# Splitting the first load of a rotary-embedding kernel into two DMAs

## The chip, the cores and the metric

One core of one Trainium2 chip. The metric is the device time of the kernel in microseconds (us); every run computes the whole reference.

## The reference

Rotary position embedding on interleaved pairs, fp32 in and out. `x` is 8 x 2048 x 16 x 64 (batch, position, head, element; 67.1 MB), `cos` and `sin` are 2048 x 32.

```python
x_pairs = x.reshape(batch, seq_len, num_heads, head_dim // 2, 2)
x1, x2 = x_pairs[..., 0], x_pairs[..., 1]
out1 = x1 * cos - x2 * sin
out2 = x1 * sin + x2 * cos
out = np.stack([out1, out2], axis=-1).reshape(batch, seq_len, num_heads, head_dim)
```

## The kernel before

One tile holds one batch. Its 2048 positions are dealt to 128 partitions, 16 (`K`) consecutive positions to each, so a partition's row is 16 x 1024 elements: 64 KB in DRAM as fp32, 32 KB on the chip as bf16. There are five such buffers (`NX`) for the eight batches.

`load` (L58) is a DMA from the GpSimd (POOL) queue that casts fp32 to bf16 on its way; `store` (L61) is one that casts back. `rotate` is three VectorE (DVE) operations on a tile: the product with the sine table into a scratch tile `qt` (L76), the product with the cosine table in place (L77), and the sum of the one and the pair-swapped other (L82).

The order of each engine's work is written out by hand (`manual_schedule`):

- SP issues three DMAs first (L86 to L88): the head, that is the first four (`HEAD`) positions of every partition's row of batch 0, as fp32 into a staging tile; then the two tables, in rows of 2 KB per partition. Much later it issues the store of the last four positions of the last batch (L126).
- POOL issues the loads at once: the other 12 positions of batch 0, batches 1 to 3 whole, and batch 4 in two parts, 14 positions and 2.
- ScalarE (ACT) casts the head to bf16 into batch 0's tile (L95). VectorE builds the tables in bf16 (L97 to L99, the sine table first), then rotates batch 0 in two parts (4 positions, 12 positions) and the others whole.
- The store of batch 0 is held back until the first part of batch 4's load has landed: ACT copies one element of it (`gate`, L112) and then one of tile 0 onto itself (L113), and the store waits for the latter. `mark` (L110) makes POOL wait in the same way for the rest of batch 4 before it stores batch 1.
- From batch 1 on, POOL issues the store of batch b and then the load of batch b + 4 into the buffer that batch b - 1 left, which waits until that batch's store has landed.
- At the end, ACT waits for batch 6's store (L124), casts the last four positions to fp32 (L125), and SP stores them.

The staging tile of the head, the scratch tile `qt` and the staging tile of the end share one buffer (tag `work`).

Of the kernel before, what the change touches and what calls it, by code (L numbers as in the profile page):

```python
# [2 lines left out]

# [4 lines left out]


@with_exitstack  # L10
def kernel(
    ctx: ExitStack,
    tc: tile.TileContext,
    x: bass.AP,
    cos: bass.AP,
    sin: bass.AP,
    out: bass.AP,
):
    nc = tc.nc
    fp32 = mybir.dt.float32  # L20
    bf16 = mybir.dt.bfloat16
    mult = mybir.AluOpType.mult
    add = mybir.AluOpType.add

    B, S, H, D = x.shape
    P = 128
    K = S // P
    KP = 16
    D2 = D // 2
    HD = H * D  # L30
    NX = 5
    HEAD = 4
    TAIL = 4
    LAST = 2


    x_t = x.rearrange("b (p k) h d -> b p k (h d)", p=P, k=K)
    out_t = out.rearrange("b (p k) h d -> b p k (h d)", p=P, k=K)
    cos_t = cos.rearrange("(p k) c -> p (k c)", p=P, k=K)
    sin_t = sin.rearrange("(p k) c -> p (k c)", p=P, k=K)  # L40

    consts = ctx.enter_context(tc.tile_pool(name="consts", bufs=1))
    xpool = ctx.enter_context(tc.tile_pool(name="xpool", bufs=NX))
    stage = ctx.enter_context(tc.tile_pool(name="stage", bufs=1))

    cos_sb = consts.tile([P, K * D2], fp32)
    sin_sb = consts.tile([P, K * D2], fp32)
    c_tab = consts.tile([P, K, D], bf16)
    s_tab = consts.tile([P, K, D], bf16)

    gate = consts.tile([1, 1], bf16)
    mark = consts.tile([1, 1], bf16)
    tiles = {}

    def load(b, k0=0, k1=K):
        if b not in tiles:
            tiles[b] = xpool.tile([P, K, HD], bf16, name="xt")
        nc.gpsimd.dma_start(out=tiles[b][:, k0:k1], in_=x_t[b, :, k0:k1])  # L58

    def store(b, k1=K):  # L60
        nc.gpsimd.dma_start(out=out_t[b, :, :k1], in_=tiles[b][:, :k1])  # L61

    def rotate(b, k0, k1):
        nk = k1 - k0
        xp = tiles[b][:, k0:k1]
        qt = stage.tile([P, KP, HD], bf16, name="qt", tag="work")

        def rows(a):
            return a.rearrange("p k (h e) -> p k h e", h=H, e=D)

        def tab(a):
            return dataclasses.replace(
                a, offset=a.offset + k0 * D, ap=[a.ap[0], [D, nk], [0, H], [1, D]]
            )

        nc.vector.tensor_tensor(out=rows(qt[:, :nk]), in0=rows(xp), in1=tab(s_tab), op=mult)  # L76
        nc.vector.tensor_tensor(out=rows(xp), in0=rows(xp), in1=tab(c_tab), op=mult)  # L77
        q_swap = dataclasses.replace(
            qt, offset=qt.offset + 1, ap=[qt.ap[0], [2, nk * HD // 2], [-1, 2]]
        )  # L80
        x3 = xp.rearrange("p k (a j) -> p (k a) j", j=2)
        nc.vector.tensor_tensor(out=x3, in0=x3, in1=q_swap, op=add)  # L82

    with tc.manual_schedule():
        head = stage.tile([P, TAIL, HD], fp32, name="st", tag="work")
        nc.sync.dma_start(out=head[:, :HEAD], in_=x_t[0, :, :HEAD])  # L86
        nc.sync.dma_start(out=cos_sb, in_=cos_t)
        nc.sync.dma_start(out=sin_sb, in_=sin_t)  # L88
        load(0, HEAD)
        for b in range(1, NX - 1):  # L90
            load(b)
        load(NX - 1, 0, K - LAST)
        load(NX - 1, K - LAST)

        nc.scalar.copy(out=tiles[0][:, :HEAD], in_=head[:, :HEAD])  # L95
        s2 = s_tab.rearrange("p k (i j) -> p (k i) j", j=2)
        nc.vector.tensor_copy(out=s2[:, :, 0], in_=sin_sb)  # L97
        nc.vector.tensor_scalar_mul(s2[:, :, 1], sin_sb, -1.0)  # L98
        nc.vector.tensor_copy(  # L99
            out=c_tab.rearrange("p k (i j) -> p (k i) j", j=2),  # L100
            in_=cos_sb.to_broadcast([P, K * D2, 2]),
        )
        for b in range(B):
            if b == 0:
                rotate(b, 0, HEAD)
                rotate(b, HEAD, KP)
            else:
                rotate(b, 0, KP)
            if b == 1:
                nc.gpsimd.tensor_copy(out=mark, in_=tiles[NX - 1][:1, K - 1, :1])  # L110
            if b == 0:
                nc.scalar.copy(out=gate, in_=tiles[NX - 1][:1, K - LAST - 1, :1])  # L112
                nc.scalar.copy(out=tiles[0][:1, 0, :1], in_=tiles[0][:1, 0, :1])  # L113
            if b < B - 1:
                store(b)

            if b >= 1 and b - 1 + NX < B:
                load(b - 1 + NX)
        store(B - 1, K - TAIL)

        tail = stage.tile([P, TAIL, HD], fp32, name="st", tag="work")
        nc.scalar.copy(out=tiles[B - 2][:1, 0, :1], in_=tiles[B - 1][:1, K - 1, :1])  # L124
        nc.scalar.copy(out=tail, in_=tiles[B - 1][:, K - TAIL :])  # L125
        nc.sync.dma_start(out=out_t[B - 1, :, K - TAIL :], in_=tail)  # L126


# [1 line left out]
_INS = ['x', 'cos', 'sin']  # L130
_OUTS = [((8, 2048, 16, 64), 'float32')]


# [23 lines left out]
```

## Time and profile before

| | us |
|---|---|
| median of three runs | 316.58 (316.47 to 316.62) |
| the profiled execution's own time | 316.51 |
| its span, first to last instruction | 314.7 |
| VectorE busy | 210.4 (67%) |
| ScalarE busy | 8.9 (3%) |
| GpSimd busy | 15.2 (5%) |
| head DMA (L86), issue to landing | 14.5 |
| cosine DMA (L87), issue to landing | 31.8 |
| sine DMA (L88), issue to landing | 51.3 |

The DMA work is in two queues: the one that GpSimd's DMAs use (q0 in the profile, software descriptors) moves 97.52 MB in 2448 packets, and the one that SP's use (q1, hardware descriptors) 4.72 MB in 576. A packet is one partition's row or one semaphore update; its bytes are counted as written, so a load that casts counts half of what it reads. Both queues run on the same 16 DMA engines, so each engine has eight rows of every DMA.

### The profile page before, as it was taken

What the parts mean: (1) busy time and instruction counts of PE and PEld (TensorE: products, weight loads), DVE (VectorE), ACT (ScalarE), POOL (GpSimd) and SP (SyncE); (2) the same over time, 40 slices, a digit from 0 to 9 for tenths busy, and PEclk for the clock granted to TensorE, in tenths of its full rate; (3) what the DMA queues carried; (4) which work ended last, traced back from release to release, by engine and by line L of the source; (5) the groups of instructions that cost most, each with busy time, mean ns of one, the idle gap of its engine ahead of it and who ended that gap; (6) DMA issues with size and microseconds to landing.
All of it is one profiled execution on the core that took longest, in us unless ns stands there. A gap on an engine that the chain in (4) does not pass through costs nothing.

```text
span 314.7 us, 130 instructions
## 1 busy us (share of the span) xinstructions
DVE 210.4 (67%) x30; ACT 8.9 (3%) x6; POOL 15.2 (5%) x22
## 2 busy tenths in 40 slices
DVE  0000002999999999999999999999999995000000
ACT  1030000000000000000000000000000000000400
POOL 4000000000001600010000000000000000000000
DMA  7999999999999999999999999999999999999997
GB/s 253 264 237 212 208 221 270 200 200 204 237 233 258 400 533 400 400 337 262 200 400 433 366 200 200 450 483 267 200 275 458 400 400 516 416 400 400 433 433 333
DMA packets 3025, 102.24 MB, mean 325 GB/s; under 512 B 337, under 2 KB 337, under 8 KB 721
## 3 DMA queue, kind: packets, MB, share of 16 engines
q0 software_dynamic: 2448, 97.52, 96.3%
q1 hardware_dynamic: 576, 4.72, 3.9%
q14 instruction: 1, 0.00, 0.0%
HBM read 67.63 MB, written 67.11 MB: 428 GB/s over the span
## 4 chain that ended last, share of the span: by engine, by line
another core or an unknown queue 87%; DMA 5%; ACT 1%; ACTq 1%; issue 0%
DMA st<-in_x_dram 5%; ACT xt L95 1%; ACTq L152 1%; ACT xt L124 0%; ACT xt L113 0%; ACTq L124 0%; ACT gate L112 0%
## 5 line engine op out<-in xcount | busy, mean ns | idle before, releaser
L77 DVE TENSOR_TENSOR xt<-xt,c_tab 128x16384 bf16<-128x16384 bf16 (+2 forms) x9 | 69.7, 7744 | 0.5
L82 DVE TENSOR_TENSOR xt<-xt,qt 128x16384 bf16<-128x16384 bf16 (+2 forms) x9 | 69.7, 7744 | 0.3
L76 DVE TENSOR_TENSOR qt<-xt,s_tab 128x16384 bf16<-128x16384 bf16 (+2 forms) x9 | 69.7, 7742 | 0.3
L97 DVE CAST s_tab<-sin_sb 128x512 bf16<-128x512 f32 x1 | 0.5, 454 | 52.9 <-DMA sin_sb<-in_sin_dram 52.9
L61 POOL DMA_DIRECT2D out_dram<-xt x8 | 4.3, 533 | 209.8 <-DVE xt L82 114.9
L58 POOL DMA_DIRECT2D xt<-in_x_dram x9 | 4.9, 562 | 38.6 <-DMA out_dram<-xt 37.8
L110 POOL COPY mark<-xt 1x1 bf16<-1x1 bf16 x1 | 5.8, 5817 | 1.3 <-DMA xt<-in_x_dram 1.3
L124 ACT COPY xt<-xt 1x1 bf16<-1x1 bf16 x1 | 0.2, 193 | 195.5 <-DMA out_dram<-xt 195.5
L95 ACT CAST xt<-st 128x4096 bf16<-128x4096 f32 x1 | 3.6, 3605 | 13.2 <-DMA st<-in_x_dram 13.2
L125 ACT CAST st<-xt 128x4096 f32<-128x4096 bf16 x1 | 3.6, 3598 | 0.0
L112 ACT COPY gate<-xt 1x1 bf16<-1x1 bf16 x1 | 0.2, 193 | 80.0 <-DMA xt<-in_x_dram 80.0
L95 ACT ACT_TABLE_LOAD x1 | 1.3, 1283 | 0.7 <-PEq L141 0.7
L99 DVE CAST c_tab<-cos_sb 128x1024 bf16<-128x1024 f32 x1 | 0.7, 685 | 0.0
L98 DVE TENSOR_SCALAR s_tab<-sin_sb 128x512 bf16<-128x512 f32 x1 | 0.4, 444 | 0.0
L113 ACT COPY xt<-xt 1x1 bf16<-1x1 bf16 x1 | 0.2, 188 | 0.0
L141 POOL MEMSET const-float32-0.0<- 128x1 f32 x1 | 0.1, 98 | 0.2 <-issue 0.2
L141 POOL MEMSET const-bfloat16-1.0<- 128x1 bf16 x1 | 0.1, 102 | 0.0
L141 POOL MEMSET const-float32-1.0<- 128x1 f32 x1 | 0.1, 98 | 0.0
L141 POOL MEMSET const-uint8-127<- 128x1 uint8 x1 | 0.1, 98 | 0.0
## 6 DMA issues: line engine op xcount, KB each, us to landing
xt<-in_x_dram POOLq DMA_DIRECT2D x6, 4096.0 KB, 57.6
out_dram<-xt POOLq DMA_DIRECT2D x1, 6144.0 KB, 46.2
xt<-in_x_dram POOLq DMA_DIRECT2D x1, 3584.0 KB, 95.4
xt<-in_x_dram POOLq DMA_DIRECT2D x1, 3072.0 KB, 21.6
st<-in_x_dram SPq DMA_DIRECT2D x1, 2048.0 KB, 14.5
out_dram<-st SPq DMA_DIRECT2D x1, 2048.0 KB, 15.5
xt<-in_x_dram POOLq DMA_DIRECT2D x1, 512.0 KB, 97.3
cos_sb<-in_cos_dram SPq DMA_DIRECT2D x1, 256.0 KB, 31.8
```

The lines of the kernel that those rows point to most:

```text
L58: nc.gpsimd.dma_start(out=tiles[b][:, k0:k1], in_=x_t[b, :, k0:k1])
L61: nc.gpsimd.dma_start(out=out_t[b, :, :k1], in_=tiles[b][:, :k1])
L76: nc.vector.tensor_tensor(out=rows(qt[:, :nk]), in0=rows(xp), in1=tab(s_tab), op=mult)
L77: nc.vector.tensor_tensor(out=rows(xp), in0=rows(xp), in1=tab(c_tab), op=mult)
L82: nc.vector.tensor_tensor(out=x3, in0=x3, in1=q_swap, op=add)
L95: nc.scalar.copy(out=tiles[0][:, :HEAD], in_=head[:, :HEAD])
L97: nc.vector.tensor_copy(out=s2[:, :, 0], in_=sin_sb)
L98: nc.vector.tensor_scalar_mul(s2[:, :, 1], sin_sb, -1.0)
L99: nc.vector.tensor_copy(out=c_tab.rearrange("p k (i j) -> p (k i) j", j=2), in_=cos_sb.to_broadcast([P, K * D2, 2]),)
L110: nc.gpsimd.tensor_copy(out=mark, in_=tiles[NX - 1][:1, K - 1, :1])
L125: nc.scalar.copy(out=tail, in_=tiles[B - 1][:, K - TAIL :])
L152: with _tile.TileContext(nc) as tc:
```

## The change

The head's DMA is replaced by two, both on SP's queue and ahead of the tables: first position 0 of every partition's row (128 rows of 4 KB, 512 KB), then positions 1 to 3 (128 rows of 12 KB, 1536 KB). They write the same staging tile; the cast at L95 still reads all four positions in one instruction and so waits for both.

```diff
     with tc.manual_schedule():
         head = stage.tile([P, TAIL, HD], fp32, name="st", tag="work")
-        nc.sync.dma_start(out=head[:, :HEAD], in_=x_t[0, :, :HEAD])
+        nc.sync.dma_start(out=head[:, :1], in_=x_t[0, :, :1])
+        nc.sync.dma_start(out=head[:, 1:HEAD], in_=x_t[0, :, 1:HEAD])
         nc.sync.dma_start(out=cos_sb, in_=cos_t)
         nc.sync.dma_start(out=sin_sb, in_=sin_t)
         load(0, HEAD)
```

## The prediction

> **What bounds the kernel now.** I read the overview of the page first, then the stretches by time, then the waits and the timeline, to see whether the first DMA sits on the path that sets the end.
>
> The DMA rows of the 40 slices:
>
> ```profile
> span 314.7 us, 130 instructions
> ...
> DVE  0000002999999999999999999999999995000000
> ...
> DMA  7999999999999999999999999999999999999997
> ...
> DMA packets 3025, 102.24 MB, mean 325 GB/s; under 512 B 337, under 2 KB 337, under 8 KB 721
> ...
> q0 software_dynamic: 2448, 97.52, 96.3%
> q1 hardware_dynamic: 576, 4.72, 3.9%
> ...
> HBM read 67.63 MB, written 67.11 MB: 428 GB/s over the span
> ```
>
> The 16 DMA engines are at 9 or more in every slice but the first and the last. VectorE works for 67% of the span, idle for six slices at the start and six at the end. The two queues together take 100.2% of 16 engines' span. The stretches, with the DMA share in the last column but one:
>
> ```profile
> core 0: us, DVE busy (x) ACT busy (x) POOL busy (x), PEclk, DMA share, GB/s
> ...
> 1.70:5.40 3.70, 0.00 (x0) 0.32 (x1) 2.86 (x6) 1.00 1.03 361
> 5.40:15.20 9.80, 0.00 (x0) 0.00 (x0) 0.00 (x0) 1.00 1.11 279
> 15.20:52.90 37.70, 0.00 (x0) 3.60 (x1) 0.00 (x0) 1.00 1.03 226
> ...
> 98.80:120.90 22.10, 22.03 (x3) 0.28 (x2) 6.89 (x3) 1.00 1.08 444
> ...
> 264.60:294.50 29.90, 0.00 (x0) 0.00 (x0) 0.53 (x1) 1.00 1.05 447
> ```
>
> The share is about 1 from 1.7 us to the last us (packets are put down to the stretch in which they start, so it can exceed 1). The kernel is as long as its packets are, laid end to end, plus 1.7 us ahead and about 1 us behind. Something that merely moves an engine's work costs nothing unless the DMA engines run dry. Where that could happen is in the timeline, where these lines stand:
>
> ```profile
> 52.93 0.45 DVE L97 CAST s_tab<-sin_sb 128x512 bf16<-128x512 f32 x1 [52.93 <-DMA sin_sb<-in_sin_dram]
> ...
> 74.37 6.56 DVE L82 TENSOR_TENSOR xt<-xt,qt 128x12288 bf16<-128x12288 bf16 x1
> ...
> 99.44 0.54 POOL L61 DMA_DIRECT2D out_dram<-xt  x1 [94.88 <-ACT xt L113]
> ...
> 107.40 0.54 POOL L61 DMA_DIRECT2D out_dram<-xt  x1 [0.26 <-DVE xt L82]
> ...
> 120.94 0.54 POOL L58 DMA_DIRECT2D xt<-in_x_dram  x1 [13.00 <-DMA out_dram<-xt]
> ...
> 264.62 0.53 POOL L61 DMA_DIRECT2D out_dram<-xt  x1 [25.65 <-DVE xt L82]
> ```
>
> VectorE starts only at 52.93, when the sine table has landed, 51.3 us after its issue. Batch 0 is rotated at 80.93, 17.9 us before the gate (98.86) lets its store go; the store of batch 1 is issued 107.40, while batch 0's flows until 120.2; the last store is issued at 264.62, while batch 6's flows until 294.5. So a later VectorE has slack, least at batch 1.
>
> Why the sine table is late is told by the trace's packet records (a record has queue, start, duration, size). One engine in the first 30 us: five head rows of 16 KB one after another, then one packet of POOL's queue (48 KB read, written as 24 KB), one head row, one POOL packet, and so on. The two queues take strict turns. Mean durations:
>
> ```
> SP queue    16 KB row 0.62 us   2 KB row 0.095   semaphore packet 0.02
> POOL queue  48 KB read 1.83     64 KB read 2.43  4 KB written (8 KB read) 0.324
> ```
>
> Each row and each semaphore packet of the SP queue thus waits for one POOL packet. After the fifth head row (POOL's first packet starts at 5.36), three head rows and a semaphore, eight cosine rows and one, eight sine rows and one are left: 22 turns, which is the 47 us to 52.9.
>
> **The change part by part.** Eight rows of 16 KB on each DMA engine become eight of 4 KB, a semaphore packet, and eight of 12 KB. The bytes are the same.
>
> DMA work: beside a POOL packet, a 16 KB row lengthens the turn by 0.616 us (turns of 2.43 against 1.814 for the POOL packet alone), a 2 KB row by 0.093 (2.505 against 2.412). So 0.0374 us per KB and 0.018 per row. Rows of 4 and 12 KB come to 0.168 and 0.467, together 0.634 against 0.616: 8 x 0.018 = 0.15 us per engine, and about 0.01 for the semaphore packet. Sum: +0.16 us, on the path, since nothing hides DMA work here.
>
> Filling the pipe: the first 16 rows took 1.0 to 1.41 us (median 1.2) against 0.62 later, 0.58 of it start-up. Small rows back to back on the SP queue are not in this trace. Below, the first row being short could give all 0.58 back; above, at the far end, all eight short rows would pay it as the first rows do, 4.6 us; but the second row of every engine already paid almost none (0.61 to 0.66 for nearly all), so I bound the loss by the same 0.58 once more. I take 0: the nearest row, POOL's 4 KB packets back to back at 0.324 us for 8 KB read, shows no start-up per packet (8 x 0.0374 = 0.30).
>
> SP: one more issue. The three now take 0.36 to 0.42 us each, at 0.74, 1.15 and 1.63; the cosine and the sine DMA are issued 0.41 later. Both wait far longer for their turn, so nothing; nothing else is queued on SP until the tail's store (298.35). If the turn no longer covered it, it would cost 0.41.
>
> Turns: until 5.36 the SP queue has the engines for itself, 3.63 us. Of that the eight short rows with start-up take 0.58 + 8 x 0.168 = 1.9, and 1.7 is left for 12 KB rows of 0.467: 3.6, so four. Four rows remain instead of three, one turn of 2.41 us more. The sine table lands at about 55.3, VectorE's whole row of work moves by 2.4 us (none if five rows fit, two turns if three fit: I take one). That is hidden by the slack: 17.9 us at batch 0, and at batch 1 the 12.8 us from 107.40 to 120.2, less 1.1 from issue to first packet (99.44 to 100.56): 11.7. At batches 2 to 7 a load or a store of 19.3 us lies queued ahead. The load of batch 5 waits for batch 0's store, not for VectorE. ScalarE's cast at L95 (3.6 us) now waits for two landings, the later near 17 us rather than 15.24; it ends before 21, and its result is wanted at 54.21. So 0.
>
> Whether the second DMA is a free-standing cost can be weighed: on one engine the head's semaphore packet starts at 14.61, and the next cosine row follows after a single POOL turn. There is no gap between DMAs of one queue. The Trainium skill, "DMA: Bandwidth & Descriptors", section on the anatomy of one DMA, gives every DMA a fixed cost of about 2.0 us; by that the sum would be +2.2, about 318.7. The trace speaks against paying it here.
>
> The sum: +0.16 on the profiled execution's 316.51 (span 314.7), 316.67; that execution is 0.07 under the median of 316.58, so 316.74 on the median.
>
> **The rivals.** *The sine table starves* (slower). The extra row turns all fall after POOL's queue has started. Each costs 2.41, and from the fifth (11.7 / 2.41 = 4.9) batch 1's store comes too late and the DMA engines idle. With all nine: VectorE 21.7 late, batch 0 done at 102.6, its store's first packets at 104.0 where the loads end at 100.9: 3.1 idle. Batch 1's store flows at 130.2, batch 0's would end at 123.3: 6.9 more, 10 in all, 326.7. For it: the waits show the tables as the only thing that VectorE waits for. Against it: 361 GB/s over 3.7 us is 1336 KB, 82 rows of 16 KB or five per engine, ahead of POOL's first packet, so most short rows must be gone by then. Chance 0.04.
>
> *A gap between the two halves* (slower). If the second half's rows began only when the first had landed, the engines would idle before POOL's start by issue to first row (0.74 to 1.73: 1.0) and last row to landing (tail: 313.54 to 313.87: 0.3). 1.3 + 0.16 gives 318.0. For it: that stretch is the only one with no second queue to fill a gap. Against: the cosine rows above. Chance 0.07. The Trainium skill's fixed cost of 2.0 us, named above, is this rival at 318.7.
>
> *Short rows fill the pipe sooner* (faster): 0.58 comes back whole, less 0.16, 316.16; only with the longest first row (1.41, so 0.79 back) is it 315.95. Chance 0.07.
>
> *The rows come out unchanged*, if software joined adjacent rows: 316.58; against it, the trace has one packet per partition row for every other DMA. Chance 0.02.
>
> **How the numbers follow.** A change of 0.2% or 0.63 us is about what a measurement can tell from none. Likeliest, 316.74, at 0.80, spread by the bounds on the start (0.58 either way), 316.2 to 317.3. Nearly all of this and of "unchanged" lies within 0.63, as does half of the faster rival; I leave 0.04 of the likeliest to slower, since its upper end is 317.3. Slower: 0.04 + 0.07 + 0.04 = 0.15. Faster: 0.05. Same: 0.80. The range, 316.2 to 317.5, takes in the likeliest case but its edges, "unchanged" and half of the faster rival, and leaves out the two slower rivals: some 0.83.
>
> **What would show it.** After: SP's queue has 128 more rows and 16 more semaphore packets, 720 packets for 576. The wait of L97 is near 55.3 instead of 52.93 and every VectorE line later by the same; the gate at L112 still ends near 98.9 (the loads do not care), and the last landing moves by 0.1 to 0.3. DMA slices stay 9 from the second to the last but one. I am wrong if a slice in the middle falls under 9, if the gate moves by over 0.6, or if the sine table lands after 64.

## The result and the profile after

The changed kernel takes 317.14 us (median of 17 runs, 317.09 to 317.24), the kernel before 316.48 in 17 runs beside it: ratio 1.0019, 95% interval 1.0012 to 1.0025, that is 0.66 us slower. The time lies in the range of the prediction (316.2 to 317.5); the forecast was +0.16, a quarter of what was measured. The profiled execution took 317.13 with a span of 315.4.

The page of the changed kernel, the lines that answer to those of before:

```profile
span 315.4 us, 134 instructions
...
DVE  0000000899999999999999999999999999000000
...
DMA  7999999999999999999999999999999999999997
...
q0 software_dynamic: 2448, 97.52, 96.2%
q1 hardware_dynamic: 720, 4.72, 4.0%
```

VectorE's row starts one slice later, and the DMA row is what it was: 9 in every slice but the first and the last. SP's queue has 720 packets for 576. So the engines were as full as before, and the span is still 0.7 us longer. The timeline shows from where on:

```profile
55.95 0.45 DVE L98 CAST s_tab<-sin_sb 128x512 bf16<-128x512 f32 x1 [55.95 <-DMA sin_sb<-in_sin_dram]
...
99.47 0.19 ACT L113 COPY gate<-xt 1x1 bf16<-1x1 bf16 x1 [76.83 <-DMA xt<-in_x_dram]
...
100.05 0.54 POOL L61 DMA_DIRECT2D out_dram<-xt  x1 [95.48 <-ACT xt L114]
...
110.42 0.54 POOL L61 DMA_DIRECT2D out_dram<-xt  x1 [0.26 <-DVE xt L82]
121.54 0.53 POOL L58 DMA_DIRECT2D xt<-in_x_dram  x1 [10.59 <-DMA out_dram<-xt]
...
267.64 0.53 POOL L61 DMA_DIRECT2D out_dram<-xt  x1 [25.64 <-DVE xt L82]
```

The gate's line before was this:

```profile
98.86 0.19 ACT L112 COPY gate<-xt 1x1 bf16<-1x1 bf16 x1 [80.00 <-DMA xt<-in_x_dram]
```

The sine table, VectorE and everything that waits for VectorE moved by 3.0 us (55.95 for 52.93, 110.42 for 107.40, 267.64 for 264.62). What waits for POOL's loads and for batch 0's store moved by 0.6: the gate 99.47 for 98.86, and the load behind batch 0's store was issued at 121.54 for 120.94. The end moved by 0.6 too (last packet 314.14 for 313.54). VectorE's 3 us vanished; the 0.6 us were there when the loads ended. They are older still, as the stretches show:

```profile
core 0: us, DVE busy (x) ACT busy (x) POOL busy (x), PEclk, DMA share, GB/s
...
1.70:5.40 3.70, 0.00 (x0) 0.00 (x0) 2.86 (x6) 1.00 1.01 328
5.40:15.20 9.80, 0.00 (x0) 0.00 (x0) 0.00 (x0) 1.00 1.09 276
```

In the 3.7 us in which SP's queue has the engines alone they moved 328 GB/s, where it was 361, at a share of 1 in both: the engines are counted busy and move less. The packet records say when. If each row's bytes (as read) are spread evenly over its own duration, the 16 engines together moved, in GB/s:

```
from, us                    3.0   3.5   4.0   4.5   5.0   5.5
before                      373   419   417   421   421   428
after                       379   406   381   356   343   355
two and two (e3, below)     420   410   421   424   425   431
head of three (e7, below)   354   399   378   388   416   431
```

The short rows come near the rate of before; it falls from 4.0 us on, while the 12 KB rows run. The records also give the size of the loss. Each DMA of POOL's queue ends with one semaphore packet on each of the 16 engines; "mean" and "last" below are over these 16:

```
                                             before    after     moved by
POOL's first packet, mean                     5.65      6.03      0.38
  moved by SP's queue until then, KB/engine   81.0      80.8
batch 4's first load part, mean              98.28     98.70      0.42
batch 4's first load part, last engine       98.50     99.10      0.60
last packet of the kernel                   313.54    314.14      0.60
```

The 0.38 at 5.65 us is lost for the same bytes. Some 0.14 of it is the row term of the prediction (7.0 rows more by then, 0.018 each, and a semaphore packet). The other 0.24 is a balance. The 12 KB rows lose 0.31 per engine: the 4.06 that ran before POOL's start took 0.544 us on average where the prediction's price is 0.467 (those between POOL's packets took 0.473). The first rows give 0.12 back: the 4 KB rows took 0.50 us per engine over their price, the five 16 KB rows before 0.62. Some 0.05 is time without a packet, in which engines had not yet started. A further 0.18 lies between the mean and the last engine. Each engine has its own eight rows of every DMA, and an engine that is behind stays behind: the last one is 0.39 us behind the mean when batch 0's load ends near 22.7 us and 0.40 at batch 4's first part (before: 0.23 and 0.22). At that point the gate waits for the last engine, and batch 0's store with it.

### The profile page after: what moved, and what is told of

Same layout as the page of the kernel before. It is cut to its first block, busy times and chain, and to the rows that moved or that the text cites. A ratio compares the mean times of both kernels' runs of the same rounds, so it can differ in the third digit from the quotient of the medians.

```text
span 315.4 us, 134 instructions
## 1 busy us (share of the span) xinstructions
DVE 210.4 (67%) x30; ACT 8.9 (3%) x6; POOL 17.6 (6%) x22
## 4 chain that ended last, share of the span: by engine, by line
another core or an unknown queue 86%; DMA 5%; ACT 2%; ACTq 1%; SPq 0%; issue 0%
DMA st<-in_x_dram 5%; ACT xt L96 1%; ACTq L153 1%; ACT L96 0%; SPq L86 0%; ACT xt L125 0%; ACT xt L114 0%; ACTq L125 0%; ACT gate L113 0%; ACTq L96 0%
## 5 line engine op out<-in xcount | busy, mean ns | idle before, releaser
L111 POOL COPY mark<-xt 1x1 bf16<-1x1 bf16 x1 | 8.2, 8240 | 1.3 <-DMA xt<-in_x_dram 1.3
```

## The experiments

Each edit is against the kernel before. Ratios are to the kernel before on the same chip, with 95% intervals.

### The long rows first (e1_long_first)

```diff
-        nc.sync.dma_start(out=head[:, :HEAD], in_=x_t[0, :, :HEAD])
+        nc.sync.dma_start(out=head[:, 0:3], in_=x_t[0, :, 0:3])
+        nc.sync.dma_start(out=head[:, 3:4], in_=x_t[0, :, 3:4])
```

> The same two DMAs in the other order: positions 0 to 2 in 12 KB rows, then position 3 in 4 KB rows. Theory A (filling the pipe: the loss of 0.66 us came because the engines start on short rows, before anything runs ahead): most of it goes, 316.6 to 316.75, and POOL's first packets start at 5.4 to 6.1 as in the kernel before. Theory B (a second DMA on the queue costs about 0.5 whatever its rows are): 317.1 as with the change. Theory C (each extra short row costs some 0.06 while the queue has the engines alone, wherever it stands): 317.1 too.

Measured: 321.98 (320.45 to 322.11), ratio 1.0161 (1.0142 to 1.0180). No theory named this, but the prediction's first rival did. Only 12 KB rows fit ahead of POOL's start (6.9 of the eight), and the 4 KB rows all took turns after it. Its timeline and stretches:

```profile
70.03 0.45 DVE L98 CAST s_tab<-sin_sb 128x512 bf16<-128x512 f32 x1 [70.03 <-DMA sin_sb<-in_sin_dram]
...
99.48 0.19 ACT L113 COPY gate<-xt 1x1 bf16<-1x1 bf16 x1 [64.56 <-DMA xt<-in_x_dram]
...
124.50 0.54 POOL L61 DMA_DIRECT2D out_dram<-xt  x1 [17.71 <-DVE xt L82]
125.03 0.54 POOL L58 DMA_DIRECT2D xt<-in_x_dram  x1
```

```profile
1.70:5.40 3.70, 0.00 (x0) 0.00 (x0) 2.87 (x6) 1.00 0.99 332
...
120.90:140.00 19.10, 19.03 (x3) 0.00 (x0) 1.07 (x2) 1.00 0.77 329
```

The sine table came 17.1 us later, seven turns. Batch 1's store was issued at 124.50, after batch 0's had drained, and the DMA share from 120.9 to 140 fell to 0.77. By the prediction's slack of 11.7 us, 17.1 late should cost 5.4; 5.46 was measured. So the order "short rows first" is what keeps the change harmless: it puts the extra rows where they need no turn. Against theory A also speaks the start: 332 GB/s in the first stretch and the gate at 99.48, 0.62 later than before, the same loss with the long rows in front.

### Nine more turns (e4_cos_in_two)

```diff
-        nc.sync.dma_start(out=cos_sb, in_=cos_t)
+        HC = K * D2 // 2
+        nc.sync.dma_start(out=cos_sb[:, :HC], in_=cos_t[:, :HC])
+        nc.sync.dma_start(out=cos_sb[:, HC:], in_=cos_t[:, HC:])
```

> The head as before in one DMA, but the cosine table in two DMAs by columns, rows of 1 KB instead of 2 KB: eight more rows and one more semaphore packet per engine, all after POOL's queue has started, so nine more turns of about 2.41 us. By the prediction's first rival the sine table lands at about 74.6 instead of 52.9 and the DMA engines idle twice for want of a store to run, 3.1 us after the loads and 6.9 after batch 0's store: 326.7. If a later VectorE is hidden farther than I reckoned, 316.7.

Measured: 324.34 (324.32 to 324.52), ratio 1.0248 (1.0234 to 1.0262).

```profile
72.57 0.45 DVE L99 CAST s_tab<-sin_sb 128x512 bf16<-128x512 f32 x1 [72.57 <-DMA sin_sb<-in_sin_dram]
...
101.12 0.54 POOL L61 DMA_DIRECT2D out_dram<-xt  x1 [96.56 <-DVE xt L82]
...
127.04 0.54 POOL L61 DMA_DIRECT2D out_dram<-xt  x1 [17.71 <-DVE xt L82]
```

```profile
120.90:140.00 19.10, 19.03 (x3) 0.00 (x0) 1.07 (x2) 1.00 0.64 274
```

Both stores now wait for VectorE, the first too (before, for the gate). The delay was 19.64 us and not 21.7: one of the nine turns fell on POOL's own semaphore packets at 61.6 to 62.2, around which the records have 32 packets of SP's queue instead of 16, two per engine. With it the slack gives 19.64 - 11.7 = 7.9; 7.8 was measured. The rival's mechanism and its threshold hold, given the delay that was measured; the forecast of 326.7 was off by that one turn.

### The second DMA alone: two and two, and half the partitions

```diff
+        nc.sync.dma_start(out=head[:, 0:2], in_=x_t[0, :, 0:2])
+        nc.sync.dma_start(out=head[:, 2:4], in_=x_t[0, :, 2:4])
```

> The head in two DMAs of 8 KB rows. As many rows as in the change, but the first are longer. Theory A: between, 316.7 to 316.95, less lost at the start than with 4 KB rows first. Theory B: 317.1. Theory C: 317.1.

Measured: 316.56 (316.44 to 317.12), ratio 1.0004 (0.9995 to 1.0013). No loss, with as many DMAs and as many rows as the change:

```profile
1.70:5.40 3.70, 0.00 (x0) 0.00 (x0) 2.87 (x6) 1.00 1.02 359
```

359 GB/s, as before. This takes theories B and C away. A's 316.7 to 316.95 was missed too, though the interval reaches into it. The sine table landed 9.6 us later (62.48), still within the slack. It also bears on the rule that the prediction weighed. The fixed cost of 2.0 us per DMA that the Trainium skill states ("DMA: Bandwidth & Descriptors", on the anatomy of one DMA) stands there in a section on DMAs issued from GpSimd, while these are issued from SP; the prediction took it for both. It does not show here for a second DMA on a busy queue: at most 0.0013 of 316.5, 0.4 us, is left for it, and 0.19 that the 8 KB rows saved at the start (they took 0.44 us per engine over their price, the 16 KB rows 0.62).

```diff
+        nc.sync.dma_start(out=head[: P // 2, :HEAD], in_=x_t[0, : P // 2, :HEAD])
+        nc.sync.dma_start(out=head[P // 2 :, :HEAD], in_=x_t[0, P // 2 :, :HEAD])
```

> The head in two DMAs of 64 partitions each, rows of 16 KB: as many rows as the kernel before, eight per engine, but one DMA and one semaphore packet more. Theory A: 316.5 to 316.65. Theory B: 317.0 to 317.2, since the second DMA is what costs. Theory C: 316.5 to 316.65, no extra rows. In all of them the sine table lands about one turn (2.4 us) later, which is hidden.

Measured: 320.22 (319.82 to 320.88), ratio 1.0118 (1.0105 to 1.0132). It was meant as a control and is none: the rows of 16 KB took 1.19 us on average before POOL's start, the first ones among them, instead of 0.74, and the engines stood at

```profile
1.70:5.40 3.70, 0.00 (x0) 0.00 (x0) 2.87 (x6) 1.00 0.96 217
```

217 GB/s. The first row started 0.37 us later (2.10 for 1.73), but the rate itself is lower: from 3 to 6 us the rows moved 203 to 256 GB/s, before 373 to 428. Two DMAs over 64 partitions each, one behind the other, ran at some 0.6 of the rate, with all engines counted busy. It says nothing on the cost of a second DMA. The sine table came 6.3 us later instead of one turn, still hidden.

### The size of the rows alone

Three positions in one DMA (`HEAD = 3`, rows of 12 KB), as many rows and DMAs as before:

```diff
-    HEAD = 4
+    HEAD = 3
```

> The head is three positions instead of four, in one DMA with 12 KB rows; the load from POOL's queue starts one position earlier and the first rotation is 3 and 13 positions. As many rows and DMAs as the kernel before. Theory D (rows of 12 KB are slow by themselves while SP's queue has the engines alone, by some 0.05 to 0.1 us a row): POOL's first packets come no earlier for the same bytes, the early rows after the first take 0.5 to 0.6 instead of 0.47, and the time is 316.8 to 317.1. Theory E (two DMAs of unequal rows drift apart and disturb each other; the size alone is harmless): early rows of 0.47, and 316.4 to 316.6.

Measured: 317.22 (317.01 to 317.43), ratio 1.0019 (1.0011 to 1.0028): the whole loss of the change without its split.

```profile
1.70:5.40 3.70, 0.00 (x0) 0.32 (x1) 2.86 (x6) 1.00 1.00 332
...
98.80:120.90 22.10, 22.00 (x4) 0.29 (x2) 2.04 (x3) 1.00 1.09 444
```

332 GB/s at the start, 444 as ever later. The last engine ended batch 4's first part 0.65 late (99.15), the mean engine 0.33. E falls: there is no second DMA here, and the loss is there. D is nearer, but its size is off: the time is above D's 316.8 to 317.1, while the early rows after the first took 0.50 us, the least that D allowed. They are not slow throughout: in the table of rates this kernel dips to 378 GB/s at 4.0 us and moves 416 from 5.0, still with 12 KB rows. Half of the lateness is the unevenness of the engines (0.65 against 0.33). And not all of the rest is in the head: POOL's rows of batch 0 are 52 KB in this kernel (1.996 us each, 0.015 over 52/48 of the 48 KB row), eight of them 0.12.

One, one and two positions:

```diff
+        nc.sync.dma_start(out=head[:, 0:1], in_=x_t[0, :, 0:1])
+        nc.sync.dma_start(out=head[:, 1:2], in_=x_t[0, :, 1:2])
+        nc.sync.dma_start(out=head[:, 2:4], in_=x_t[0, :, 2:4])
```

> The head in three DMAs: one position in 4 KB rows, one more in 4 KB rows, two in 8 KB rows. Sixteen rows and two semaphore packets per engine more than the kernel before, and no row of 12 KB. Theory D: only the rows' own 0.018 us each, 316.6 to 316.9, although it has more short rows at the start than the change. Theory E: 317.1 or more. Theory A (short rows at the start cost): 317.2 or more. The sine table lands some three turns later (7 us), which is hidden.

Measured: 317.32 (317.16 to 317.48), ratio 1.0023 (1.0015 to 1.0032). It has no 12 KB row and loses more, so D as "12 KB alone" is too narrow. The time is what E and A had named, but E had fallen with the head of three and A with the long rows first. Of the 0.50 that its mean engine is late at batch 4, the rows themselves are 0.3 (16 x 0.018 and two semaphore packets); the other 0.2 goes with rows that ran over their price at the start (0.89 us per engine, before 0.62), and the last engine is late by 0.77. The sine table came 10.6 us later instead of 7, still hidden.

A last set tried a rule that would cover both: rows of an odd number of 4 KB. One DMA each, `HEAD` = 2, 5, 6 and 8 (the staging tile made as large as the head).

> A head of two positions in one DMA of 8 KB rows (POOL's load takes the other 14). Theory G (rows of an odd number of 4 KB, as 4, 12 and 20, leave the engines stalled and uneven while SP's queue has them alone; rows of 8, 16 and 24 do not): no loss, 316.3 to 316.55, since 8 KB rows filled the pipe sooner in the two-and-two run. Theory H (the loss is how the rows' ends happen to meet the start of POOL's queue, with no rule by size): anything from 316.3 to 317.3. VectorE starts much earlier, which gains nothing by itself.

> A head of five positions in one DMA of 20 KB rows. Theory G: a loss as with 12 KB rows, 317.0 to 317.4, and the last engine's share of the loads ends 0.4 to 0.7 us later than in the kernel before. Theory H: no rule, and if all that counts is the number of rows (eight), 316.5 to 316.6.

> A head of six positions in one DMA of 24 KB rows. Theory G: no loss, 316.4 to 316.6. Theory H: no rule. If larger heads as such cost (more bytes on the slower-starting queue), more than with five positions.

> A head of eight positions in one DMA of 32 KB rows. Theory G: no loss, 316.4 to 316.6. Theory H: no rule. The sine table lands two or three turns later than before (58 to 61), which is hidden.

```
head                  row KB     time    ratio (interval)            batch 4: mean, last engine
2 (e9_head_two)       8          316.48  0.9998 (0.9989 to 1.0007)   -0.13  -0.04
two and two (e3)      8, 8       316.56  1.0004 (0.9995 to 1.0013)   +0.01  +0.03
4 (before)            16         316.5                                0      0
6 (e11_head_six)      24         316.68  1.0006 (0.9997 to 1.0014)   +0.04   0.00
8 (e12_head_eight)    32         316.60  1.0001 (0.9992 to 1.0010)   +0.05  +0.13
5 (e10_head_five)     20         316.77  1.0008 (0.9999 to 1.0017)   +0.17  +0.20
the change            4, 12      317.14  1.0019 (1.0012 to 1.0025)   +0.42  +0.60
3 (e7_head_three)     12         317.22  1.0019 (1.0011 to 1.0028)   +0.33  +0.65
one, one, two (e8)    4, 4, 8    317.32  1.0023 (1.0015 to 1.0032)   +0.50  +0.77
```

The last column, how late the slowest engine ends batch 4's first part, tells the time within 0.1 us in all but one (six positions, 0.17; there the profiled execution took 316.52, which it tells to 0.01); the mean is off by up to 0.34. The four kernels with rows of 8, 24 and 32 KB alone are within noise of the one before. Those with rows of 4 and 12 KB lose 0.6 to 0.8. Rows of 20 KB were expected at 317.0 to 317.4 and came to 316.77: the sign of the rule, not its size, and the interval still holds no change. Six positions came out 0.08 above their range too. So the rule of odd multiples is not shown; a loss that shrinks as odd rows grow longer would fit as well, and theory H, no rule by size, is not ruled out.

### The tables first

```diff
-        nc.sync.dma_start(out=head[:, :HEAD], in_=x_t[0, :, :HEAD])
         nc.sync.dma_start(out=cos_sb, in_=cos_t)
         nc.sync.dma_start(out=sin_sb, in_=sin_t)
+        nc.sync.dma_start(out=head[:, :HEAD], in_=x_t[0, :, :HEAD])
```

> The two tables' DMAs are issued ahead of the undivided head. VectorE then waits for the head: seven or eight rows of 16 KB and a semaphore at one POOL packet each, some 20 us, so it starts near 25 us instead of 53. By the prediction's reading that gains nothing, since the DMA engines are busy all the time: 316.4 to 316.7. If VectorE's start were what sets the end: 290 to 300. It is also the base for the same with the head divided.

Measured: 317.22 (316.21 to 318.72), ratio 1.0020 (1.0005 to 1.0035). In the profile (an execution of 318.72):

```profile
4.19 0.45 DVE L97 CAST s_tab<-sin_sb 128x512 bf16<-128x512 f32 x1 [4.19 <-DMA sin_sb<-in_sin_dram]
...
30.12 2.29 DVE L76 TENSOR_TENSOR qt<-xt,s_tab 128x4096 bf16<-128x4096 bf16 x1 [24.54 <-ACT xt L95]
```

The first rotation starts at 30.12 instead of 54.21, and the kernel gains nothing: VectorE's start does not set the end. The median is above the expected 316.4 to 316.7, in a wide spread.

The same with the head divided as in the change:

> The tables first, and then the head as in the change (4 KB rows, then 12 KB rows). Only the short rows run before POOL's queue starts; the 12 KB rows take turns with POOL's packets. Theories D and E: no loss from the 12 KB rows there (0.467 each), so the undivided head with the tables first plus 0.1 to 0.2. If the second DMA cost about 0.5 wherever it stands: plus 0.5 to 0.7.

Measured: 316.90 (316.75 to 318.34), ratio 1.0018 (1.0007 to 1.0029). Both kernels scatter by over 1.5 us from run to run, so a difference of 0.1 to 0.2 between them can't be seen, and with these intervals (0.0015 and 0.0011 of 316.5 either way) even the 0.5 to 0.7 of a costly second DMA is unlikely rather than excluded; the ratios, 1.0018 and 1.0020, show no loss.

These two and the half partitions widen the test of the last column above. Their profiled executions took 318.72, 318.34 and 320.44, that is 2.21, 1.83 and 3.93 more than the profiled execution before. Their last engine ended batch 4's first part 2.17, 1.82 and 3.92 late, the mean engine only 0.69, 0.37 and 3.26. The slowest engine at the end of the loads sets the time.

## Why the prediction was right, and the term that was off

- **The bound.** Right: the DMA engines stay full, and what moves on VectorE alone is hidden. It started 3.0 us later in the changed kernel and about 24 earlier with the tables first, and neither set the time.
- **The turns.** Right: one extra turn was reckoned, sine table near 55.3; it came at 55.95. The rest of the way is the 0.6 us of the start.
- **The slack.** Right, and tested beyond the change: with the delays that were measured, 11.7 us gives +5.4 and +7.9 for the two kernels that exceed it; +5.46 and +7.82 were measured. The rival was real and only its condition was not met.
- **The row term.** 0.16 for eight rows and a semaphore packet; not seen by itself. Two and two has the same extra packets, and its mean engine is only 0.01 late, with rows that took 0.44 us over the price ahead of POOL's start where the 16 KB rows took 0.62.
- **Filling the pipe.** This is the term that was mis-sized. I took 0, bounded at 0.58 either way. The short rows at the front did behave as priced: counted up to 3 us, they took 0.52 us per engine over the price, the 16 KB rows 0.59. (Of the "first 16 rows" that the prediction read, 15 took 1.0 to 1.41 and one 0.61.) But I carried the 12 KB rows at 0.467, a price from rows that alternate with POOL's packets, into the stretch where they run alone, and there they took 0.544. And I summed means, where the last engine counts: 0.60 late for a mean of 0.42. Together 0.24 + 0.18, which with the 0.16 of the rows is 0.58 of the 0.60.
- **What would show me wrong.** I had written that the gate must not move by over 0.6 and the last landing only by 0.1 to 0.3. The gate moved by 0.61 and the end by 0.6; by these marks the sum of 0.16 was wrong. With +0.66 against a bound of 0.63, "within 0.2%", which I gave 0.80, is a coin's toss, and the range held because its bounds on the start were wide, not because the sum was close.
- **The gap between the halves.** It did not happen: two and two would show it and has none.

What stays open is why rows of 12 KB, and to a lesser degree 4 and perhaps 20 KB, stall and spread the engines while SP's queue runs alone, and rows of 8, 16, 24 and 32 KB don't. The records don't name the engine or the address of a packet, and no run changed the 64 KB from the start of one partition's row to the next. No version beat the kernel before: the best, a head of two positions, is at 0.9998 (0.9989 to 1.0007).

## What to carry to other kernels

When the DMA engines are full from end to end, price an edit in packets and not in engines: what its rows add, and above all how many rows stand ahead of a transfer that something waits for, since each costs a turn of the other queue. Work out the delay at which that wait surfaces, because below it the cost is nothing and above it every microsecond counts. A price taken from rows that alternate with another queue does not hold where the queue runs alone, and the end was set by the slowest of 16 engines, not by their mean.

## What the runs showed of the hardware that was not expected

- Two DMAs over 64 of 128 partitions each moved 217 GB/s at the start of the kernel, where one with the same rows over 128 moved 361, with all engines counted busy. The Trainium skill ("DMA: Bandwidth & Descriptors", rules for kernel authors) says not to divide a transfer into disjoint partition halves, because they serialize; the trace agrees with the advice, but serializing alone does not account for it: the rate itself fell, and the kernel was 3.7 us slower.
- With two landings to wait for, ScalarE's table load slid behind the first of two waits, the one for the second landing (17.66 us): it ran at 17.73 us instead of 0.73, 1.28 us on the way to the cast. It lay far from the path.
- POOL's one-element copy (`mark`) took 5.82 us before, 8.24 after and 0.96 with a head of three; each time it ended within 0.05 us of the end of the VectorE operation that was running. Where VectorE's phase shifts, so does POOL's release.
